# A hybrid SSD and stick-breaking decoder on one core: tiles of 256 tokens behind the attention, 512-column down products, and convolutions that end in their PSUM bank

## The chip, the cores and the metric

The kernel runs on one core of one Trainium2 chip. The metric is the device time of one execution in microseconds (us). It is given as the median of three runs. The profile is of one execution of its own, whose time stands beside the others below.

The engines are named as the profile names them: PE is TensorE (matmuls), PEld its weight loads, DVE is VectorE, ACT is ScalarE, POOL is GpSimd, SP is SyncE (it issues most of the DMAs here).

## The reference

Everything is float32. The stream is 16 learned meta tokens and then 1024 tokens, 1040 in all, of width 1024.

```
h = concat(meta, x)                                        # 1040 x 1024
h = h + ssd_mixer(rmsnorm(h));   h = h + conv_ffn(rmsnorm(h))      # layer 0
k, v = rmsnorm(h) @ w_kv                                   # shared, 16 heads of 64
h = h + stick_breaking_attention(rmsnorm(h) @ w_q, k, v) @ w_o     # layer 1
h = h + conv_ffn(rmsnorm(h))
out = rmsnorm(h)[16:]                                      # the meta tokens are dropped

def conv_ffn(u):                                           # D_FF = 2816
    y = u @ w_up                                           # 2 x 2816 columns
    y = w[0]*y[t-2] + w[1]*y[t-1] + w[2]*y[t] + bias       # causal, 3 taps along the tokens
    g, val = split(y)
    return (silu(g) * val) @ w_down
```

What is returned covers tokens 16 to 1039. The last place where a token mixes with others is the convolution of layer 1's feed-forward part, which looks two tokens back. So behind the attention the result depends on tokens 14 to 1039 alone.

## The kernel before, in words

Tokens lie along the free axis and channels along the 128 partitions, eight channel blocks for the width of 1024. Every float32 product is made of three float32r matmuls (`mm3`, lines 152 to 157): operand and weight are each split into a high and a low part, and high by high, high by low and low by high are added up in one PSUM bank. ACT makes the high parts (a copy with rounding), DVE the operands' low parts and POOL the weights' low parts (both a subtraction with two SBUF inputs).

The stages, in order of time: the mixer of layer 0; `out_proj`, which adds its output to the stream; the feed-forward part of layer 0; the attention; `o_proj`; the feed-forward part of layer 1; the final norm. A feed-forward part has these steps:

- `enter_ffn` (line 726) adds the last part of the projection to the stream in four tiles of `FN` = 260 tokens, squares each row for the norm, and stores the stream in HBM. `forms` (line 804) then makes the normed operands. Both layers work on 1040 tokens. Columns 0 and 1 of each row stand for the two tokens ahead of the first and are zero.
- `up` (line 863) multiplies by a Strassen-like scheme: seven products instead of eight for each of 22 blocks b (a block of gate columns and one of value columns) and each half t of the tokens. Each product is 12 matmuls of 262 columns (a tile and two tokens of halo). The two halves go step by step beside each other. A block holds three PSUM banks, x, y and z. Products 0, 2 and 3 begin them, and DVE adds parts into them in place (line 898). Products 1, 4, 5 and 6 are then accumulated on top. `conv` (line 273) ends each of the four results: ACT multiplies the first tap and adds the bias, and two DVE instructions add the other taps, from the bank into an SBUF tile `c`. For the gate a Silu on ACT follows. `done` (line 889) multiplies gate by value, both in SBUF, on DVE (line 890) and stores the result by DMA. After product 4 the bank y is copied to an SBUF tile by ACT (line 912), and DVE adds two SBUF tiles (line 898) before that result's convolution.
- `down` (line 936) is a Strassen-like scheme as well: two rounds of seven products i, each over two sets of weight rows. For each product `operands` (line 972) makes sums of the stored tiles on DVE and POOL, and splits them (lines 993 to 996). `part` (line 1001) writes eight results, two token tiles t of 260 by four blocks f, into all eight PSUM banks (`kinds`, line 999). The first set starts the eight banks, the second set is accumulated on top, and then `add` (line 1036) takes each bank into an SBUF accumulator, on DVE or, for some first ones, on ACT. Behind the seven products come the last 6 of the 22 weight rows as plain products in four tiles of 260 tokens, and behind each tile `after` is called.
- For layer 1 `after` is `finish` (line 1396): after tiles 1, 2 and 3 it normalises 348, 348 and 344 tokens in chunks of 116 tokens. Each chunk is transposed on PE (eight 128-row blocks, line 1409), scaled on DVE, ACT and POOL, and stored in one DMA whose SBUF side has 116 partitions (112 for the last, 100 for the first) of 4 KB each (line 1448). For the last 344 tokens the sum of squares is taken from the transposed rows (lines 1422 to 1436).

The order of each engine's instructions in these stages is chosen at build time by a scheduler with a model of the times. The attention and the mixer have an order written out by hand. The change touches neither of the two.

Of the kernel before, what the change touches and what calls it, by code (L numbers as in the profile page):

```python
# [13 lines left out]
P = 128  # L14
# [15 lines left out]
FN = 260  # L30
HB = 2
FW = 264

# [35 lines left out]
class Trunk:  # L69
# [99 lines left out]
    def split_half(self, t, s):  # L169

        x = self.Q(s, F32R)
        hi, lo = x[:, : L // 2], x[:, QW // 2 : QW // 2 + L // 2]
# [100 lines left out]
    def conv(self, ps, out, n, taps, halo, wcol, bcol, between=lambda: None):  # L273
# [5 lines left out]
        for i in range(1, taps):  # L279
            nc.vector.scalar_tensor_tensor(out, ps[:, o + i : o + i + n], wcol(i), out, op0=ALU.mult, op1=ALU.add)  # L280
# [94 lines left out]
    def accumulate(self, h, f, s0, n, w, ks, front=0, bank=None, base=0):  # L375

        ps = (bank or (self.ex if f % 3 == 2 else self.mm))("acc")
        c, o = slice(s0 - base, s0 - base + n), slice(front + s0, front + s0 + n)
# [328 lines left out]
    def out_proj(self, hd, ys, yd, pool):  # L707
# [3 lines left out]
        for g in range(3):  # L711
            ops = [self.split(ys[g][q] if yd[g] is None else self.fetch(yd[g][q], "y"), "y") for q in range(4)]
            for f in range(KD):
# [3 lines left out]
                for s0, n in TT:  # L717
                    self.accumulate(h, f, s0, n, lambda i, f: (w[0][:, i * P : i * P + P], w[1][:, i * P : i * P + P]), ops, HB)
        ops = [[self.split_half(ys[3][q][:, L // 2 * x : L // 2 * (x + 1)], "y") for q in range(4)] for x in range(2)]
        ws = [self.load_wd(a["w_out"][12 + i], pool if i < 2 else None) for i in range(4)]  # L720
        return self.enter_ffn(0, h, [(ws, o) for o in ops], pool)
# [4 lines left out]
    def enter_ffn(self, layer, h, last, pool):  # L726


        nc = self.nc
        r = self.rp.tile([P, QW], F32, tag="r", name=self.nm("r"))  # L730
        nc.gpsimd.tensor_copy(r[:, :HB], self.zero[:, :HB])
        d = self.dp.tile([KD, P, L], F32, tag=f"hm{layer}", name=f"hm{layer}")
# [3 lines left out]
        def tile(j, work):  # L736
            ws, ops = last[j // 2]
            ms[j] = self.sm("ms")
            for f in range(KD):
                self.accumulate(h, f, FN * j, FN, lambda i, f: (ws[i][0][:, f * P : f * P + P], ws[i][1][:, f * P : f * P + P]), ops, HB, next(banks), L // 2 * (j // 2))  # L740
                self.square_row(ms[j], h, j, f)
# [3 lines left out]
        def factors(j):  # L745

            c = r[:, HB + FN * j : HB + FN * j + FN]
            b, ps = self.tmp("y")[:, :FN], ms.pop(j)[:, :FN]
# [9 lines left out]
        def rest():  # L758
            forms.append(form_tiles())
            yield from self.forms(h, r, 1, f"ffn_norm{layer}", forms[1][1:], pool)  # L760

        def form_tiles():
# [3 lines left out]
            for x in wide[1]:  # L766
                nc.gpsimd.memset(x.bitcast(F32)[:, HB + 2 * FN : 2 * FW], 0.0)
            own = {i: (self.Q("bh", F32R), self.Q("bl", F32R)) for i in (0, 2, 3, 4, 6)}
            out = {i: [tuple(x[:, k * FW : k * FW + HB + FN] for x in own[i]) for k in range(KD // 2)] for i in own}
            both = [tuple(x[:, k % 2 * 2 * FW : k % 2 * 2 * FW + HB + 2 * FN] for x in wide[k // 2]) for k in range(KD // 2)]  # L770
            out[1] = [tuple(x[:, : HB + FN] for x in hl) for hl in both]
            out[5] = [tuple(x[:, FN :] for x in hl) for hl in both]
            return out, out, both

        def store(x):
            for k in range(KD):
                nc.sync.dma_start(d[k, :, L // 2 * x : L // 2 * (x + 1)], h[k][:, HB + L // 2 * x : HB + L // 2 * (x + 1)])
# [7 lines left out]
        work = self.forms(h, r, 0, f"ffn_norm{layer}", forms[0][1:], pool)  # L785
# [8 lines left out]
    def square_row(self, ms, h, j, f):  # L794

        q = self.tmp("sq")[:, :FN]
        self.nc.scalar.activation(q, h[f][:, HB + FN * j : HB + FN * j + FN], AF.Square)
        self.nc.tensor.matmul(ms[:, :FN], self.ones, q, start=f == 0, stop=f == KD - 1, skip_group_check=True)
# [5 lines left out]
    def forms(self, h, r, t, gain, tiles, pool):  # L804


        nc = self.nc
        N, N2 = HB + FN, HB + 2 * FN
        tt = nc.vector.tensor_tensor
        out, both = tiles  # L810
        s = slice(2 * FN * t, 2 * FN * t + N2)

        new = slice(s.start + HB * t, s.stop)
        for k in range(KD // 2):
# [8 lines left out]
            b11, b12, b21, b22 = b1[:, :N], b1[:, FN:], b2[:, :N], b2[:, FN:]  # L823
# [39 lines left out]
    def up(self, layer, w0, forms, rest, pool):  # L863

        nc = self.nc
        tt = nc.vector.tensor_tensor
        N = HB + FN
# [668 lines left out]
```

## Time and profile before

| | us |
|---|---|
| median of three runs | 3050.51 |
| lowest and highest of them | 3044.32, 3052.45 |
| the profiled execution: its own time | 3047.2 |
| its span, first to last instruction | 3045.5 |

From the trace, the stages run from about 683 to 881 us (`out_proj` with the entry of layer 0's feed-forward part), 912 to 1357 (up, layer 0), 1357 to 1546 (down, layer 0), 1639 to 2176 (the heads of the attention), 2176 to 2312 (`o_proj` and the entry), 2312 to 2756 (up, layer 1), 2756 to 3019 (down, layer 1) and 3019 to 3045.5 (end of the final norm, and the stores).

How to read the views: the page and the groups give busy time of an engine and the mean duration of one instruction. A matmul's duration includes its passage through the array, and matmuls overlap, so what one costs in a row of many is the time of a stretch divided by their number. A table of windows gives the busy time of each engine in chosen stretches, the number of its instructions in brackets, the granted PE clock, and what share of the 16 DMA engines was busy. In a group's last column stands idle time ahead of its instructions and what ended it.

### The profile page before, as it was taken

The page shows a single profiled execution, that of the slowest core. Times are in us where ns is not written, and L with a number is a line of the kernel's source. Part 1 is how long each engine was busy: PE and PEld are TensorE (multiplying, and loading weights), DVE is VectorE, ACT ScalarE, POOL GpSimd, SP SyncE. Part 2 cuts the span into 40 slices and gives each one's busy share as a digit, 9 for nine tenths or more (in the row PEclk, how much of TensorE's full clock was granted, in tenths as well). Part 3 has the DMA queues.
Part 4 walks back from the last instruction along what each step waited for, and adds up shares of the span by engine and source line. Part 5 has one row for each costly group of instructions (what it writes and reads, how often), then busy time and mean ns, then how long its engine had stood idle before and what let it go on. Part 6 is the DMA issues. An engine that isn't in the chain of part 4 may idle for free.

```text
span 3045.5 us, 58682 instructions
## 1 busy us (share of the span) xinstructions
PE 2890.8 (95%) x22535; PEld 2779.1 (91%) x22535; DVE 2336.8 (77%) x4030; ACT 1646.9 (54%) x3403; POOL 1414.2 (46%) x1289
## 2 busy tenths in 40 slices
PE   8999999989989999999999999999998999998996
PEld 5998998889979999999999999999897999998996
DVE  5686868875378888788877888888759877888874
ACT  4555555553246555554335877777645565555332
POOL 1254444532316767657723222222335766666741
PEclk9999999999989999999999999999998999999998
DMA  5243323313212222244132222212431222225231
GB/s 160 74 119 86 110 79 112 111 59 126 80 71 70 79 78 78 83 159 142 50 106 76 63 66 62 57 54 56 150 111 56 74 81 83 77 86 182 71 98 56
DMA packets 125534, 273.42 MB, mean 90 GB/s; under 512 B 15782, under 2 KB 55334, under 8 KB 125254
## 3 DMA queue, kind: packets, MB, share of 16 engines
q1 hardware_dynamic: 119942, 258.74, 27.3%
q10 hardware_dynamic: 4048, 6.36, 0.6%
q0 software_dynamic: 1264, 4.57, 0.4%
q8 instruction: 177, 2.90, 0.4%
q14 instruction: 103, 0.84, 0.1%
HBM read 201.26 MB, written 53.45 MB: 84 GB/s over the span
## 4 chain that ended last, share of the span: by engine, by line
PE 69%; DVE 17%; ACT 5%; issue 5%; POOL 2%; DMA 2%; SPq 0%; POOLq 0%; ACTq 0%; DVEq 0%
PE p L155 9%; PE p L156 9%; PE p L157 9%; PE acc L155 5%; PE pj L155 5%; PE acc L156 5%; PE acc L157 5%; PE pj L156 5%; PE pj L157 5%; DVE gl L996 3%; PE po L1301 2%; PE lg L1259 2%; PE wT L1286 1%; DVE kp L1272 1%; DVE bl L818 1%
## 5 line engine op out<-in xcount | busy, mean ns | idle before, releaser
L155 PE MATMUL pj<-uh,wh 128*128 128x348 f32 (+2 forms) x1536 | 507.5, 331 | 15.9 <-DVE qs L1210 7.1
L156 PE MATMUL pj<-ul,wh 128*128 128x348 f32 (+2 forms) x1536 | 498.9, 325 | 0.0
L157 PE MATMUL pj<-uh,wl 128*128 128x348 f32 (+2 forms) x1536 | 495.6, 323 | 0.0
L156 PE MATMUL p<-bl,fh 128*128 128x262 f32 x1408 | 401.1, 285 | 14.0 <-DVE bl L818 14.0
L155 PE MATMUL p<-bh,fh 128*128 128x262 f32 x1408 | 401.7, 286 | 1.8 <-ACT fh L849 1.4
L157 PE MATMUL p<-bh,fl 128*128 128x262 f32 x1408 | 399.2, 285 | 0.0
L850 POOL TENSOR_TENSOR fl<-x,fh 128x1024 fp32r<-128x1024 f32 x88 | 213.2, 2423 | 352.2 <-ACT fh L849 306.5
L155 PEld LDWEIGHTS pj<-uh,wh 128*128 128x128 f32 x1536 | 291.9, 190 | 23.3 <-DVE qs L1210 9.2
L149 POOL TENSOR_TENSOR wl<-w,wh 128x1024 fp32r<-128x1024 f32 (+2 forms) x80 | 164.1, 2054 | 320.3 <-ACT wh L148 320.1
L156 PE MATMUL p<-bl,wh 128*128 128x262 f32 x1056 | 303.2, 287 | 8.8 <-DVE bl L818 8.8
L155 PE MATMUL p<-bh,wh 128*128 128x262 f32 x1056 | 301.8, 287 | 6.2 <-ACT bh L817 6.2
L157 PE MATMUL p<-bh,wl 128*128 128x262 f32 x1056 | 301.9, 286 | 0.0
L156 PEld LDWEIGHTS pj<-ul,wh 128*128 128x128 f32 x1536 | 292.7, 191 | 1.5 <-issue 0.7
L157 PEld LDWEIGHTS pj<-uh,wl 128*128 128x128 f32 x1536 | 291.9, 190 | 0.2
L280 DVE SCALAR_TENSOR_TENSOR c<-p,params,c 128x260 f32<-128x260 f32 x528 | 251.3, 484 | 48.3 <-ACT c L277 38.5
L156 PEld LDWEIGHTS p<-bl,fh 128*128 128x128 f32 x1408 | 266.9, 190 | 16.0 <-DVE bl L818 15.9
L155 PE MATMUL acc<-gh,wh 128*128 128x260 f32 x896 | 260.5, 291 | 22.1 <-DVE p L1041 10.8
L155 PEld LDWEIGHTS p<-bh,fh 128*128 128x128 f32 x1408 | 267.1, 190 | 4.2 <-ACT fh L849 1.9
L156 PE MATMUL acc<-gl,wh 128*128 128x260 f32 x896 | 259.1, 289 | 11.3 <-DVE gl L996 11.2
L157 PEld LDWEIGHTS p<-bh,fl 128*128 128x128 f32 x1408 | 266.6, 190 | 0.1
L890 DVE TENSOR_TENSOR c<-c,c 128x260 f32<-128x260 f32 x176 | 254.2, 1445 | 6.4 <-ACT c L886 3.4
L157 PE MATMUL acc<-gh,wl 128*128 128x260 f32 x896 | 257.9, 289 | 0.1
(309 smaller groups left out, 8557.4 us busy)
## 6 DMA issues: line engine op xcount, KB each, us to landing
w<-in_w_up SPq DMA_DIRECT2D x88, 512.0 KB
g<-c SPq DMA_DIRECT2D x176, 130.0 KB
w<-in_w_down SPq DMA_DIRECT2D x44, 512.0 KB
w<-in_w_in SPq DMA_DIRECT2D x40, 512.0 KB
b<-g SPq DMA_DIRECT2D x32, 520.0 KB
E<-ea_d SPq DMA_DIRECT2D x32, 464.0 KB
D<-acs_d SPq DMA_DIRECT2D x32, 420.5 KB
h<-h_d SPq DMA_DIRECT2D x16, 520.0 KB
```

The lines of the kernel that those rows point to most:

```text
L149: nc.gpsimd.tensor_tensor(wl[:, :n], w32[:, :n], wh[:, :n].bitcast(F32), op=ALU.subtract)
L155: mm(out, wh, uh, start=first, stop=False, skip_group_check=joins)
L156: mm(out, wh, ul, start=False, stop=False, skip_group_check=joins)
L157: mm(out, wl, uh, start=False, stop=last, skip_group_check=joins)
L280: nc.vector.scalar_tensor_tensor(out, ps[:, o + i : o + i + n], wcol(i), out, op0=ALU.mult, op1=ALU.add)
L818: tt(hl[1], x, hl[0].bitcast(F32), op=ALU.subtract)
L850: tt(lo[:, :n], t, hi[:, :n].bitcast(F32), op=ALU.subtract)
L890: self.last_up = tt(g[:, :FN], g[:, :FN], v[:, :FN], op=ALU.mult)
L996: tt(gl, x, gh.bitcast(F32), op=SUB)
L1259: nc.tensor.matmul(ps[:nt, :m], part[:, c0 : c0 + nt], ks[a][:, s0 : s0 + m], start=x == 0, stop=x == 1)
L1272: nc.vector.tensor_tensor_scan(rev, rev, self.one[:nt].to_broadcast([nt, m + 1]), init, ALU.mult, ALU.mult)
L1301: nc.tensor.matmul(po[64 * a : 64 * a + 64, w], v[: CH[c][1], c, 64 * a : 64 * a + 64], wt[a][: CH[c][1], c, :nt], start=x == 0, stop=x == ...
```

## The change

`FN` becomes `FNS = (260, 256)`, one tile size for each layer's feed-forward part. For layer 0 the tiles stay as they are. For layer 1:

- `o_proj` and everything behind it work on tokens 14 to 1039 (`ORG` = 14). The two columns of halo ahead of the first tile are now tokens 14 and 15 themselves. Tiles are of 256 tokens. In `enter_ffn` the first one has 258. The products of `up` have 258 columns.
- In `down` the two token tiles of 256 become one product of 512 columns (`parts`). Each product i then takes four banks, and `kinds` is cycled, so that consecutive products use different halves of the eight banks.
- `finish` works on 256 tokens, two chunks of 128 tokens, after tile 1 twice, and after tiles 2 and 3. Chunks have 128 partitions. For the last tile all four scalings are on DVE, and each chunk is stored in two DMAs of 512 columns, each behind its own scaling.

For both layers, in `up`: after product 4 DVE adds the bank and the SBUF tile directly, without the copy on ACT. The convolutions of products 5 and 6 end in their own bank (Silu writes it, or the last tap does), and `done` multiplies that bank by an SBUF tile.

```
-FN = 260
+FNS = (260, 256)
+ORG = META - HB
...
-    def conv(self, ps, out, n, taps, halo, wcol, bcol, between=lambda: None):
+    def conv(self, ps, out, n, taps, halo, wcol, bcol, between=lambda: None, last=None):
...
         for i in range(1, taps):
-            nc.vector.scalar_tensor_tensor(out, ps[:, o + i : o + i + n], wcol(i), out, op0=ALU.mult, op1=ALU.add)
+            to = out if last is None or i + 1 < taps else last
+            nc.vector.scalar_tensor_tensor(to, ps[:, o + i : o + i + n], wcol(i), out, op0=ALU.mult, op1=ALU.add)
...
# enter_ffn
-        nc.gpsimd.tensor_copy(r[:, :HB], self.zero[:, :HB])
+        edges = [0] + [HB + F * j for j in range(1, 5)]
+        if layer == 0:
+            edges[0] = HB
+            nc.gpsimd.tensor_copy(r[:, :HB], self.zero[:, :HB])
+        tiles = [(x, y - x) for x, y in zip(edges, edges[1:])]
...
# up
-            def conv(x, i, c):
-                o = self.tmp("c")
-                self.conv(x, o[:, :FN], FN, 3, HB, lambda q: self.par(cw, (KF * i + b) * 3 + q), self.par(cb, KF * i + b))
+            def conv(x, i, back=False):
+
+                o = self.tmp("c")[:, :F]
+                back = x[:, :F] if back else None
+                self.conv(x, o, F, 3, HB, lambda q: self.par(cw, (KF * i + b) * 3 + q), self.par(cb, KF * i + b), last=back if i else None)
                 if i == 0:
-                    nc.scalar.activation(o[:, :FN], o[:, :FN], AF.Silu)
-                return o
-
-            def done(g, v, j):
-                self.last_up = tt(g[:, :FN], g[:, :FN], v[:, :FN], op=ALU.mult)
-                nc.sync.dma_start(d[b, :, FN * j : FN * j + FN], g[:, :FN])
+                    nc.scalar.activation(o if back is None else back, o, AF.Silu)
+                return o if back is None else back
+
+            def done(o, x, y, j):
+                self.last_up = tt(o, x, y, op=ALU.mult)
+                nc.sync.dma_start(d[b, :, F * j : F * j + F], o)
...
-            u3 = copy(product(4, y, False))
-            add(p5, p5, u3)
-            v1 = conv(p5, 1, 1)
+            add(p5, product(4, y, False), p5)
+            v1 = conv(p5, 1)
             yield
-            done(conv(product(5, z, False), 0, 1), v1, 2 * t + 1)
+            done(v1, conv(product(5, z, False), 0, True), v1, 2 * t + 1)
             yield
-            done(g0, conv(product(6, y, False), 1, 0), 2 * t)
+            done(g0, conv(product(6, y, False), 1, True), g0, 2 * t)
...
# down
-        H, S = D // 2, L // 2
+        H, S = D // 2, 2 * F
+        parts = [(0, S)] if S <= 512 else [(0, F), (F, F)]
...
-        kinds = (self.mm, self.sm, self.lg, self.sm, self.mm, self.sm, self.lg, self.ex)
+        kinds = cycle((self.mm, self.sm, self.lg, self.sm, self.mm, self.sm, self.lg, self.ex))
...
-                for n, (t, f) in enumerate((t, f) for t in range(2) for f in range(4)):
+                for t, f in ((t, f) for t in range(len(parts)) for f in range(4)):
                     if x == 0:
-                        ps[t, f] = kinds[n]("acc")
+                        ps[t, f] = next(kinds)("acc")
...
# o_proj
+        spans = (ORG, META + 2 * F), (META + 2 * F, L)
...
-            h[f] = self.fetch(hd[f], "h", front=HB)
+            h[f] = self.Q("h")
+            self.nc.sync.dma_start(h[f][:, : L - ORG], hd[f, :, ORG:])
...
# finish
+        for i in ((0, 1), (2,), (3,))[j]:
+            self.finish_tile(h, i)
...
+        n = FNS[1]
+        s0, last = n * j, j == 3
+        chunks = [(i, s0 + P * i) for i in range(n // P)]
...
-                if b and i < 2:
-                    nc.scalar.activation(y[:m, w], p[:m], AF.Copy, scale=r[:m, i : i + 1])
-                    nc.gpsimd.tensor_tensor(y[:m, w], y[:m, w], self.gfin[:m, w], op=ALU.mult)
+                if b and not last:
+                    nc.scalar.activation(y[:, w], p, AF.Copy, scale=r[:, i : i + 1])
+                    nc.gpsimd.tensor_tensor(y[:, w], y[:, w], self.gfin[:, w], op=ALU.mult)
                 else:
-                    nc.vector.scalar_tensor_tensor(y[:m, w], p[:m], r[:m, i : i + 1], self.gfin[:m, w], op0=ALU.mult, op1=ALU.mult)
-            s = META if t0 == 0 else 0
-            nc.sync.dma_start(out[t0 + s - META : t0 + m - META, :], y[s:m, :])
+                    nc.vector.scalar_tensor_tensor(y[:, w], p, r[:, i : i + 1], self.gfin[:, w], op0=ALU.mult, op1=ALU.mult)
+                if last:
+                    nc.sync.dma_start(out[t0 : t0 + P, w], y[:, w])
+            if not last:
+                nc.sync.dma_start(out[t0 : t0 + P, :], y)
```

More of the change, by code (lines that the diff above doesn't have):

```diff
@@ L759, in rest @@
             forms.append(form_tiles())
-            yield from self.forms(h, r, 1, f"ffn_norm{layer}", forms[1][1:], pool)
+            yield from self.forms(h, r, 1, layer, forms[1][1:], pool)
         def form_tiles():
@@ L784, in enter_ffn @@
         w0 = self.up_weights(layer, 0, pool)
-        work = self.forms(h, r, 0, f"ffn_norm{layer}", forms[0][1:], pool)
+        work = self.forms(h, r, 0, layer, forms[0][1:], pool)
         for j in (2, 3):
@@ L1400, in finish @@
             nc.sync.dma_start(self.gfin, self.a["final_norm"].to_broadcast([P, D]))
[L1401 to L1402 removed]
+        n = FNS[1]
+        s0, last = n * j, j == 3
+        chunks = [(i, s0 + P * i) for i in range(n // P)]
         ss = self.small("fs")
[L1404 to L1406 removed]
+        banks = cycle((self.lg, self.mm) if last else (self.sm,))
@@ L1438, in finish @@
+            nc.vector.tensor_tensor(ss[:, :2], s2[:, 0], s2[:, 1], op=ALU.add)
+            r = self.token_rstd(ss, P, 2)
+        for i, t0 in chunks:
             y = self.Q("y")[:, :D]
```

142 lines of the change are left out of this document (73 added, 69 removed).

## The prediction

> **What bounds the kernel now.** I read the page first, then a table of windows by stage, then the groups with their forms, then single rows.
>
> ```profile
> span 3045.5 us, 58682 instructions
> PE 2890.8 (95%) x22535; PEld 2779.1 (91%) x22535; DVE 2336.8 (77%) x4030; ACT 1646.9 (54%) x3403; POOL 1414.2 (46%) x1289
> PE 69%; DVE 17%; ACT 5%; issue 5%; POOL 2%; DMA 2%; SPq 0%; POOLq 0%; ACTq 0%; DVEq 0%
> ```
> PE is busy nearly all the time and makes up most of the chain; DVE is second. Where each of them binds is seen by stage:
>
> ```profile
> core 0: us, PE busy (x) PEld busy (x) DVE busy (x) ACT busy (x) POOL busy (x), PEclk, DMA share, GB/s
> 690.00:815.00 125.00, 123.37 (x772) 121.52 (x771) 62.75 (x122) 34.82 (x63) 34.69 (x26) 1.00 0.29 100
> 912.00:1355.00 443.00, 442.00 (x3631) 440.57 (x3630) 364.04 (x587) 259.71 (x537) 289.78 (x165) 1.00 0.28 87
> 1357.00:1536.00 179.00, 162.37 (x1284) 159.50 (x1283) 150.13 (x136) 72.78 (x97) 134.75 (x46) 0.96 0.33 106
> 2176.00:2281.00 105.00, 104.82 (x822) 102.34 (x823) 58.11 (x130) 40.91 (x83) 27.32 (x19) 1.00 0.37 129
> 2281.00:2312.00 31.00, 16.75 (x78) 14.24 (x77) 30.86 (x47) 13.85 (x32) 13.90 (x8) 0.67 0.13 43
> 2312.00:2756.00 444.00, 443.16 (x3629) 442.05 (x3628) 362.51 (x587) 260.43 (x534) 290.18 (x165) 1.00 0.27 89
> 2756.00:2936.00 180.00, 163.79 (x1295) 161.12 (x1293) 152.69 (x137) 72.77 (x97) 134.13 (x46) 0.96 0.31 104
> 2936.00:3019.00 83.00, 83.00 (x701) 82.82 (x700) 47.05 (x96) 19.67 (x34) 14.12 (x10) 1.00 0.17 53
> 3019.00:3046.00 27.00, 3.57 (x31) 3.08 (x29) 7.95 (x20) 5.09 (x11) 3.05 (x2) 0.62 0.23 74
> ```
> The stages `out_proj` (first row), `o_proj` (fourth) and both up stages (second and sixth) are full of matmuls: PE busy for 442 of 443 and 443.2 of 444 us. There only fewer PE cycles help, and what DVE or ACT save is worth nothing. The down stages (third and seventh) leave PE idle for 16 to 17 us. Into the norm at 2281 to 2312 DVE leads, and in the last 27 us nothing is busy for long. So the change has to be costed separately in each.
>
> **Narrower tiles, layer 1.** A matmul of 262 columns costs 443.16 / 3629 = 122.1 ns in a row of many (sixth row), one of 348 or 344 columns (346.7 on average) 123.37 / 772 = 159.8 ns (first row). That is 0.445 ns a column. Four columns less save 1.78 ns. The matmuls that it meets, from the code: `o_proj` 480 and its last part in the entry 288, up 22 blocks x 2 halves x 7 products x 12 = 3696, and the six last down rows 576, together 5040, all in stretches that PE fills. 5040 x 1.78 = 9.0 us. The ends are close: 9.4 us if all of the cost goes with the columns, about 7 if the first tile's 258 and waits between products take some back. The DVE-led 31 us shrink with the columns by 4 of 262, 0.5 us.
>
> **Products of 512 columns in layer 1's down stage.** There are 1344 matmuls of 260 columns (2 rounds x 7 x 2 sets x 8 x 6), and there will be 672 of 512. Two of 260 cost 2 x 121.2 = 242.4 ns. By the line through the two rows one of 512 costs 122.1 + 250 x 0.445 = 233.4. The ends are 227.8 (the slope alone, no fixed part) and 238.6 (all in proportion). I take 233.4, as the line holds through 346.7. That is 672 x 9 = 6.0 us of PE time, with ends of 2.6 and 9.8.
>
> The Trainium skill (TensorE: Matmul & The Clock Gate, Back-to-back issue gap) has N / 2.4 + 2.5 ns for a matmul behind another. By it a product of 512 costs 215.8 ns and two of 256 cost 218.3, so joining them would bring next to nothing; the trace disagrees, with 122.1 ns at 262 columns where the rule has 111.7. With 215.8 against the measured pair the sum would have 17.9 us in place of 6.0.
>
> How much of the 6.0 shows depends on what PE waits for in that stage, and on how long DVE takes there:
>
> ```profile
> L155 PE MATMUL acc<-gh,wh 128*128 128x260 f32 x447 | 129.8, 290 | 10.7 <-DVE p L1041 5.4 <-DVE h L1041 3.0 <-DVE c L280 2.2
> L156 PE MATMUL acc<-gl,wh 128*128 128x260 f32 x447 | 128.9, 288 | 5.5 <-DVE gl L996 5.4
> ```
> ```profile
> 2757.00:2805.00 48.00, 40.32 (x303) 39.30 (x302) 46.40 (x19) 23.95 (x41) 43.27 (x14) 0.93 0.29 97
> 2850.00:2897.00 47.00, 41.63 (x339) 40.80 (x338) 45.79 (x46) 17.14 (x17) 41.49 (x13) 0.98 0.04 12
> ```
> PE waits 16 us in all: 8.4 for a bank that DVE has not yet added up (L1041), 2.2 for one that a last convolution still reads (L280), 5.4 for a low part (L996). In the first half of each round (95 us) DVE is busy for 46.4 of 48 and 45.8 of 47 us and leads; in the rest PE does. In the PE-led 84 us the wider products bring 6.0 x 84 / 179 = 2.8 us, and the four free banks end the 3.0 us of waits for `h`. In the DVE-led part only DVE's savings count. They come from here:
>
> ```profile
> L890 DVE TENSOR_TENSOR c<-c,c 128x260 f32<-128x260 f32 x176 | 254.2, 1445 | 6.4 <-ACT c L886 3.4
> L898 DVE TENSOR_TENSOR ft<-ft,ft 128x262 f32<-128x262 f32 x88 | 86.0, 977 | 0.1
> L898 DVE TENSOR_TENSOR p<-p,ft 128x262 f32<-128x262 f32 x176 | 72.9, 434 | 61.2 <-ACT ft L895 60.4 <-PE p L157 0.7
> L1041 DVE TENSOR_TENSOR h<-h,acc 128x260 f32<-128x260 f32 x112 | 42.8, 416 | 11.2 <-PE acc L157 11.2
> L630 DVE TENSOR_TENSOR state<-state,S 128x512 f32<-128x512 f32 x28 | 19.0, 679 | 3.7 <-POOL state L629 3.7
> ```
> The same amount of work takes 1445 or 977 ns with both inputs in SBUF and 434 or 416 with one in PSUM. What stretches it is seen at the turn from up to down, first DVE, then POOL:
>
> ```profile
> 2758.43 4.95 DVE L890 TENSOR_TENSOR c<-c,c 128x260 f32<-128x260 f32 x2 [1.68 <-ACT c L886]
> 2763.30 1.00 DVE L280 SCALAR_TENSOR_TENSOR c<-p,params,c 128x260 f32<-128x260 f32 x2
> 2764.33 1.56 DVE L890 TENSOR_TENSOR c<-c,c 128x260 f32<-128x260 f32 x1
> 2765.81 2.38 DVE L979 TENSOR_TENSOR b<-b,b 128x1040 f32<-128x1040 f32 x2
> ```
> ```profile
> 2758.16 2.40 POOL L994 TENSOR_TENSOR wl<-w,wh 128x1024 fp32r<-128x1024 f32 x1 [18.40 <-ACT wh L993]
> 2760.53 2.55 POOL L978 TENSOR_TENSOR w<-w,w 128x1024 f32<-128x1024 f32 x1
> 2763.05 2.56 POOL L994 TENSOR_TENSOR wl<-w,wh 128x1024 fp32r<-128x1024 f32 x1
> ```
> Each multiply ends where a POOL subtraction ends (2760.5, 2763.1, 2765.6). With an input in PSUM they don't wait for POOL.
>
> **The turn from up to down.** The three last multiplies take 6.5 us and would take 3 x 0.42, so DVE comes to its first sum (L979) up to 5.2 us earlier, in both layers. In layer 0 that is all that is gained. PE cannot use all of it, since POOL's three subtractions end at 2765.6 as before: I take 4 us, between 0 and 5.2. In layer 1 the DVE-led part gets the 5.2, and from the second round's four products in it 4 x (8 x 0.416 - 4 x 0.679) = 2.5 us, and 0.5 from 1024 columns in place of 1040. Sum for layer 1's down stage: 2.8 + 3.0 + 5.2 + 2.5 + 0.5 = 14. Waits that end for one reason come back in part as waits for the low parts, so I take 12, between 4 and 17.
>
> **The up stages themselves.** Of a layer's 88 multiplies each sheds 1.0 us of DVE, of its 44 additions each 0.55, and 44 copies leave ACT. All of it lies beside PE, which has no idle time to give: 0. What could cost something is that banks y and z are now held until the multiply. `s` and `t` go in turns, 14 products of 12 x 0.122 = 1.46 us for a pair. Bank y of `s` is released behind its product 6 (13th place) and is taken again, with three buffers, 15 products after its product 2 (18th place): four products, 5.9 us, lie between. The chain in it is ACT 0.57, two taps of 0.48 and a multiply of 0.42, some 2 us. z has more room. So 0; below is the price if the cover is gone. Nothing is queued behind these waits on PE but the next product 2.
>
> **The end.** Only the last tile's norm and stores lie behind the last matmul:
>
> ```profile
> 3019.78 0.43 DVE L382 TENSOR_TENSOR h<-h,acc 128x260 f32<-128x260 f32 x1 [1.73 <-PE acc L157]
> 3021.48 1.29 DVE L1430 COPY copy<-fin 116x512 f32<-116x512 f32 x2 [1.28 <-PE fin L1409]
> 3025.43 0.16 DVE L1435 TENSOR_TENSOR fs<-fs 128x3 f32<-128x3 f32 x1
> 3027.10 2.07 DVE L1446 SCALAR_TENSOR_TENSOR y<-fin,ty,gfin 116x512 f32<-116x512 f32 x3
> ```
> ```profile
> 3029.20 3.54 SPq L1448 DMA_DIRECT2D out<-y  x3
> ```
> ```profile
> 2273.00:2275.00 2.00, 2.00 (x17) 1.94 (x17) 2.00 (x7) 0.72 (x3) 0.00 (x0) 1.00 0.77 294
> 3030.00:3044.00 14.00, 0.00 (x0) 0.00 (x0) 0.00 (x0) 0.00 (x0) 0.95 (x1) 0.50 0.34 100
> ```
> ```profile
> 2922.26 3.72 DMA g<-g
> ```
> Two chunks in place of three take a copy and a square from DVE (0.65 each): L1435 comes at 3024.1 instead of 3025.4. The small chain to the first scaling takes 1.7 as before: 3025.8. Four scalings of 0.69 end at 3028.6. Stores of 116 and 112 partitions run at 100 GB/s in the last 14 us with 0.34 of the DMA engines; the stream's stores of 128 partitions (2273 to 2275) run at 294 GB/s with 0.77. So the last 256 KB, issued at 3028.9, take about what a read of 260 KB over 128 partitions takes, 3.7 us: 3032.6. With 1 us for the close (an estimate: 14 us at 100 GB/s are the 1.4 MB stored and end at about 3044, the span at 3045.5) it is 3033.5 instead of 3045.5: 12 us less. SP's ten stores instead of nine cost nothing, as its first six are issued beside matmuls. Eight transposes less save 0.9 us of PE (0.11 each).
>
> **Sum.** 9.0 + 0.5 + 12 + 4 + 12 + 0.9 = 38 us. The span goes from 3045.5 to 3007, the profiled execution from 3047.2 to 3009. The median is 3.3 above that execution: 3050.5 - 38 = 3012.5.
>
> **Rivals.**
> - Slower: the banks of the up stages. If the multiply into y ends later than the 5.9 us after product 6, PE waits once for each of 42 blocks and layer. From 0.45 us of lateness on (84 x 0.45 = 38) all is given back; 1 us gives 3012.5 + 84 = 3096. Against it: the chain of 2 us, and a DVE that gets freer. 5%.
> - The down stage stays with DVE and POOL: their subtractions go on in turns, PE's 16 us of waits only change place, and layer 0 gains nothing. Then 16 of the 38 shrink to 3: 3025. For it: POOL's 43.3 of 48 us. 20%.
> - The end: 100 GB/s belongs to the output tensor, not to 116 partitions. Then 1 MB takes 10.5 us from 3027 on and the end saves 7 instead of 12: 3017. 10%. The Trainium skill (DMA: Bandwidth & Descriptors, Why a DMA increments its semaphore by 16 and not by 1) says that a DMA uses the largest number of engines up to 16 that divides its outer dimension. By it 116 partitions use 4, and 128 use 16; no run here has yet shown it for this output.
> - A product of 512 columns costs 216 ns, with a fixed part that vanishes: 672 x 17.4 more PE time goes, half of it in the PE-led part: 3007. 5%.
>
> **How the numbers follow.** My forecast has 60%: 3012, with its own range of 3004 to 3020 from the ends of the terms. With the rivals the range is 2998 to 3032: the lower end takes the upper ends of all the terms and the cheap product, the upper end the second and third rival together. What a measurement can tell from no change is 0.3%, 9 us. All but the first rival lie under 3041: faster 0.93, the same 0.03, slower 0.04.
>
> **What would show it.** In the changed profile: up of layer 1 shorter by 6.6 us and that of layer 0 by none, PE still full in both; L890 near 420 ns; about 672 products of 512 columns, at about 233 ns in a full stretch; waits for L1041 nearly gone; behind the last product 14 us instead of 26, with stores that use most DMA engines. I would be wrong if PE waited for DVE inside the up stages, or if the down stage kept its 180 us.

## The result, and the profile after

The changed kernel takes 3025.11 us (median of four runs, 3024.58 to 3029.16) against 3050.51: a ratio of 0.9924, with an interval of 0.9909 to 0.994. (The 3050.51 is a median of four runs as well, and not of three.) It is 25 us faster, where 38 were predicted.

The page of the kernel after, in the lines that answer to those of before:

```profile
span 3023.1 us, 57199 instructions
PE 2875.1 (95%) x21855; PEld 2733.1 (90%) x21855; DVE 2158.8 (71%) x3994; ACT 1621.9 (54%) x3308; POOL 1403.3 (46%) x1282
PE 52%; DVE 13%; ACT 4%; issue 3%; DMA 2%; POOL 0%; SPq 0%; DVEq 0%; ACTq 0%; POOLq 0%
```
DVE lost 178 us of work, POOL 11, PE 16. Only 22.4 us of span went between the two profiled executions (3 us less than between the medians, so 3 of the 25 us stand in no row below), and most of DVE's saving lay beside PE. Where the span went is seen by stage. The table of windows after, cut at the first and last matmul of each stage (busy us of each engine, instructions in brackets, then granted clock, DMA share, GB/s); in order: layer 0's seven products; its last six weight rows with the way to the attention's heads; `o_proj`; the entry; up; layer 1's seven products; its last six rows; the end.

```profile
1356.70:1544.00 187.30, 168.84 (x1347) 166.36 (x1346) 155.74 (x148) 74.50 (x100) 139.37 (x48) 0.96 0.32 107
1544.00:1641.30 97.30, 92.12 (x696) 89.75 (x695) 62.99 (x108) 34.50 (x69) 24.82 (x19) 0.96 0.26 86
2178.00:2281.60 103.60, 103.44 (x819) 101.13 (x819) 56.68 (x128) 40.19 (x83) 26.63 (x19) 1.00 0.37 128
2281.60:2312.00 30.40, 16.11 (x80) 13.46 (x78) 30.26 (x45) 13.22 (x28) 14.31 (x8) 0.66 0.15 49
2312.00:2752.90 440.90, 438.95 (x3634) 438.02 (x3635) 271.22 (x592) 248.74 (x494) 283.83 (x165) 1.00 0.27 90
2752.90:2925.90 173.00, 160.65 (x674) 127.02 (x673) 157.29 (x99) 70.05 (x82) 136.72 (x46) 0.98 0.31 103
2925.90:3011.50 85.60, 80.19 (x652) 79.57 (x651) 52.91 (x102) 22.64 (x46) 18.64 (x15) 0.96 0.17 67
3011.50:3023.10 11.60, 1.64 (x16) 1.40 (x13) 6.58 (x17) 3.07 (x7) 0.00 (x0) 0.74 0.24 90
```
The same stages before, cut in the same way:

```profile
1356.10:1544.70 188.60, 171.34 (x1346) 168.47 (x1345) 157.03 (x150) 75.49 (x101) 138.34 (x48) 0.95 0.34 110
1544.70:1639.10 94.40, 91.02 (x694) 88.92 (x693) 63.50 (x108) 34.31 (x69) 24.41 (x19) 0.98 0.27 88
2175.80:2280.40 104.60, 104.42 (x822) 101.84 (x819) 57.71 (x130) 40.30 (x83) 26.72 (x19) 1.00 0.37 127
2280.40:2312.00 31.60, 17.35 (x82) 14.84 (x81) 31.46 (x49) 14.45 (x32) 14.50 (x8) 0.68 0.14 49
2312.00:2756.30 444.30, 443.46 (x3632) 442.35 (x3631) 362.77 (x588) 260.43 (x534) 290.18 (x165) 1.00 0.27 89
2756.30:2942.70 186.40, 170.19 (x1347) 167.34 (x1346) 157.14 (x146) 75.11 (x100) 136.53 (x47) 0.96 0.32 106
2942.70:3019.60 76.90, 76.90 (x652) 76.90 (x651) 42.34 (x87) 17.33 (x31) 11.72 (x9) 1.00 0.14 45
3019.60:3045.50 25.90, 2.97 (x26) 2.48 (x24) 7.95 (x20) 5.09 (x11) 3.05 (x2) 0.61 0.24 75
```
Row by row, before less after: +1.3 and -2.9 in layer 0's down stage, +1.0 `o_proj`, +1.2 the entry, +3.4 up of layer 1, +13.4 its seven products, **-8.7 its last six rows**, +14.3 the end. That is 23.0; the stages not shown give -0.6. (Of the -2.9 about half or less repeats: `e3_two_of_256` and `e10_last_product_256` below, with the same layer 0, take 95.9 and 95.5 us there.) The row to explain is the seventh: 652 matmuls that PE did without a gap before now take 8.7 us longer. PE's waits there, by line and releaser (us in all, times, longest), after:

```profile
PE acc L156 <- DVE h L1054: 3.4, 2, 2.0
PE acc L158 <- POOL wl L1063: 2.0, 1, 2.0
```
Before, the same view is empty. The waits bring 5.4 us; the rest goes with the clock, 0.96 in that row against 1.00 (last section).

### The profile page after: what moved, and what is told of

It reads as the page before. It is cut to its first block, busy times and chain, and to the rows that moved or that the text cites. A ratio compares the mean times of both kernels' runs of the same rounds, so it can differ in the third digit from the quotient of the medians.

```text
span 3023.1 us, 57199 instructions
## 1 busy us (share of the span) xinstructions
PE 2875.1 (95%) x21855; PEld 2733.1 (90%) x21855; DVE 2158.8 (71%) x3994; ACT 1621.9 (54%) x3308; POOL 1403.3 (46%) x1282
## 4 chain that ended last, share of the span: by engine, by line
PE 52%; DVE 13%; ACT 4%; issue 3%; DMA 2%; POOL 0%; SPq 0%; DVEq 0%; ACTq 0%; POOLq 0%
PE p L156 9%; PE p L157 9%; PE p L158 9%; PE acc L157 4%; PE acc L156 4%; PE acc L158 4%; DVE gl L1007 3%; PE po L1314 2%; PE pj L156 2%; PE pj L158 2%; PE pj L157 2%; PE lg L1272 1%; DVE kp L1285 1%; PE wT L1299 1%; ACT kp L1275 1%
## 5 line engine op out<-in xcount | busy, mean ns | idle before, releaser
L157 PE MATMUL p<-bl,fh 128*128 128x262 f32 (+1 forms) x1408 | 401.0, 285 | 14.0 <-DVE bl L827 14.0
L156 PE MATMUL p<-bh,fh 128*128 128x262 f32 (+1 forms) x1408 | 401.3, 286 | 4.2 <-ACT fh L858 3.5
L158 PE MATMUL p<-bh,fl 128*128 128x262 f32 (+1 forms) x1408 | 399.3, 284 | 0.0
L157 PE MATMUL p<-bl,wh 128*128 128x262 f32 (+1 forms) x1056 | 301.8, 286 | 8.5 <-DVE bl L827 8.5
L156 PE MATMUL p<-bh,wh 128*128 128x262 f32 (+1 forms) x1056 | 301.9, 286 | 6.3 <-ACT bh L826 6.3
L158 PE MATMUL p<-bh,wl 128*128 128x262 f32 (+1 forms) x1056 | 301.2, 285 | 0.0
L282 DVE SCALAR_TENSOR_TENSOR c<-p,params,c 128x260 f32<-128x260 f32 (+1 forms) x440 | 207.9, 481 | 94.4 <-ACT c L278 92.6
L157 PE MATMUL acc<-gl,wh 128*128 128x260 f32 (+1 forms) x672 | 217.9, 326 | 19.8 <-DVE gl L1007 19.8
L384 DVE TENSOR_TENSOR h<-h,acc 128x256 f32<-128x256 f32 (+4 forms) x232 | 102.6, 450 | 175.1 <-PE acc L158 172.5
L156 PE MATMUL acc<-gh,wh 128*128 128x260 f32 (+1 forms) x672 | 215.0, 325 | 8.7 <-DVE p L1054 5.4
```

The lines of the kernel that those rows point to most:

```text
L156: mm(out, wh, uh, start=first, stop=False, skip_group_check=joins)
L157: mm(out, wh, ul, start=False, stop=False, skip_group_check=joins)
L158: mm(out, wl, uh, start=False, stop=last, skip_group_check=joins)
L282: nc.vector.scalar_tensor_tensor(to, ps[:, o + i : o + i + n], wcol(i), out, op0=ALU.mult, op1=ALU.add)
L384: self.nc.vector.tensor_tensor(h[f][:, o], h[f][:, o], ps[:, :n], op=ALU.add)
```

## The experiments

**Which half of the change acts.** Two kernels take it apart. `e1_convs_only` is the kernel before with the new `up` alone (`conv` with `last`, no copy, `done` with a bank); `e2_tiles_only` is the kernel after with the old `up` and its copy.

> The kernel before with the PSUM convolutions alone, in both layers, tiles as before. Theory (DVE reaches its first sum of the down stage 5 us earlier, but then takes turns with POOL and the low parts come no earlier): 3049 to 3051 of 3050.5, no change; L890's successor near 430 ns, L979's successor 5 us earlier in both layers, PE's waits in the two down stages still 15 to 17 us each. Rival (what the prediction had: the head start reaches PE): 4 to 5 us less in each layer, 3041.

> The changed kernel with the convolutions as before (copies, multiplies in SBUF), tiles of 256, 512-column products and the new end kept. Theory: 3024 to 3028, the same as the changed kernel within 3 us, since the up stages are full of matmuls and the turn gives nothing. Rival (the convolutions carry part of the gain): 3033 or more.

Measured: `e1_convs_only` 3048.63 us, ratio 1.0002 (0.9993 to 1.0012); `e2_tiles_only` 3025.29, ratio 0.9927 (0.9913 to 0.9942). Neither theory is contradicted: the gain comes from the tiles, the products and the end. The convolutions that end in PSUM take nearly all of the 92 us that DVE lost in layer 1's up stage (362.8 to 271.2 in the rows above), and nothing that shows from the kernel.

**The wide products alone.** The kernel after, with products of two times 256 columns again:

```
-        parts = [(0, S)] if S <= 512 else [(0, F), (F, F)]
+        parts = [(0, F), (F, F)]
```


> The changed kernel with two products of 256 columns in place of one of 512 in layer 1's down stage, all eight banks for each product. Theory: the seven-product part gets 5 to 8 us longer (672 x 9 ns, and waits for banks), and 3 to 5 us of the waits in the last six rows go, as PE comes there later: 3027 to 3029. Rival (the wide products cause the waits, with adds of 0.68 us): the last six rows lose all 8.7 us that they had gained, and the kernel comes to 3020 or less.

Measured: 3025.51 us, ratio 0.9921 (0.9905 to 0.9938): no difference to after. The seven products of `e3_two_of_256` and its last rows:

```profile
2751.20:2935.90 184.70, 165.53 (x1346) 163.05 (x1346) 152.95 (x145) 74.27 (x100) 139.62 (x47) 0.97 0.32 104
2935.90:3012.80 76.90, 76.49 (x652) 76.28 (x651) 45.89 (x95) 21.49 (x44) 14.94 (x13) 1.00 0.14 56
```
The products of 512 columns do save 11.7 us in the first row (184.7 to 173.0), and lose 8.7 in the second (76.9 to 85.6). The gain is real, and most of it is given back at once. Theory and rival each had one half: the rows get all of their 8.7 us back, as the rival said, but the products lose more than the 5 to 8 us of the theory, so the kernel stays above the rival's 3020.

**The end.** The kernel before, with only its stores cut so that most of each has 112 partitions (seven times sixteen), and the other 4 follow:

```
-            nc.sync.dma_start(out[t0 + s - META : t0 + m - META, :], y[s:m, :])
+            for a, b in ((s, 112), (112, m)) if m > 112 else ((s, m),):
+                nc.sync.dma_start(out[t0 + a - META : t0 + b - META, :], y[a:b, :])
```


> The kernel before with each store of 116 partitions cut into one of 112 and one of 4. Theory (the number of partitions sets how many DMA engines work): the last stores use most engines, about 300 GB/s instead of 100, and the time behind the last matmul falls from 26 to 17 or 18 us: 3042. Rival (100 GB/s belongs to the output): 3050 or a little more.

Measured: 3035.97 us, ratio 0.996 (0.9946 to 0.9975), and 17.2 us behind the last matmul instead of 25.9. The trace puts 8.7 us of the gain there, as the theory had it; the 2.4 us of span besides lie in stages that the edit leaves alone. The DMA view of the last microseconds, 40 slices each: first the kernel before (slices of 0.44 us), then `e4_store_112` (0.36), then after (0.35):

```profile
DMA  0000135799733343222313222232222211010000
GB/s 0 0 0 0 66 84 159 178 243 215 131 94 75 103 122 94 84 84 94 56 66 94 94 94 94 103 112 94 84 103 103 84 66 56 37 47 9 0 0 0
```
```profile
DMA  0000000000000000000009997999999976200000
GB/s 0 0 0 0 0 0 0 0 0 0 0 0 0 0 0 0 0 0 0 0 0 319 307 273 262 296 307 307 273 273 296 353 307 239 80 23 0 0 0 0
```
```profile
DMA  0000000000000000000000000002999999960000
GB/s 0 0 0 0 0 0 0 0 0 0 0 0 0 0 0 0 0 0 0 0 0 0 0 0 0 0 0 105 392 375 380 375 375 381 386 228 0 0 0 0
```
The first digit row sits at 2 to 3 tenths of the 16 engines for most of the way, the other two at 9. (Its hump of up to 243 GB/s was not taken apart; the last of its three stores has 112 partitions.) Before and in `e4_store_112` it is the same tensor in the same rows of 4 KB, and only the cut by partitions differs: some 95 GB/s with 116, some 300 with 112. After, with 128 and rows of 2 KB, it is 380. The rival, that the slow rate belongs to the output, falls. The Trainium skill (DMA: Bandwidth & Descriptors, Why a DMA increments its semaphore by 16 and not by 1) gives the largest divisor up to 16: 4 engines for 116, 16 for 112 and 128; the trace agrees, with 2 to 3 tenths of the engines busy in the one case and 9 in the others.

**Why the last six rows lose 8.7 us: first tries.** I took POOL's late low parts and DVE's sums at that place for the cause, each curable by itself: `e5a_stage_only` gives every second of the six weight rows a staging buffer of its own, `e5b_sums_later` has the program write the sums (L1024) one for each row product in the first tile, and two in the second; `e5_stage_and_sums` does both.

```
+            if b % 2:
+                w32 = pool.tile([P, QW], F32, tag="x32", name=self.nm("x32"), bufs=2)[:, :D]
...
-                for _ in range(2 if j == 0 else 1):
+                for _ in range(2 if j == 1 else 1):
```


> The changed kernel, and in both layers' down stages every second of the last six weight rows is staged in the other tile kind (x32) instead of all in the three of w32, and the second share of the sums of accumulators is taken one tile later. Theory (the last six rows wait for their weights' low parts, which queue for staging tiles and take turns with DVE, and for adds that queue behind the sums): layer 1's last six rows fall from 85.6 to 77 to 80 us, the kernel to 3016 to 3020. Rival (the loss there has another cause, the halved clock at any short wait, or the width of the adds alone): 3024 or more.

> The changed kernel with the second kind of staging tile alone. Theory: PE's wait of 2.0 us for a weight's low part at the head of the last six rows goes, with one interval of half clock: 3 to 4 us of the 8.7, kernel about 3021. Rival (POOL's pace, not the staging, sets it): 3024 to 3026, the wait as before.

> The changed kernel with the later sums alone. Theory: the waits for banks that DVE has not added up (1.4 and 2.0 us, with an interval of half clock) go: 3 to 5 us, kernel about 3021. Rival (the adds are late because of the low parts ahead of them, not the sums): 3024 to 3026.

Measured: 3027.16, 3026.3 and 3025.48 us, ratios 0.9933 (0.9916 to 0.9949), 0.9929 (0.9914 to 0.9944) and 0.9928 (0.9913 to 0.9944). None differs from after: all three theories missed, and the times are about those of their rivals. In `e5a_stage_only` PE's waits stayed (3.5 us for `h`, 2.1 for POOL's low part), so a staging buffer of its own is no cure. In `e5b_sums_later` the scheduler put the sums where they had been, so it tested nothing, and `e5_stage_and_sums` only the staging: here, writing the sums later in the program did not move them.

**Whether DVE and POOL bind the seven products.** The kernel after without POOL's sums of weight tiles in `operands`; it leaves these four sums out of each set, in both layers:

```
-                    pt(a21, a11, a21, op=SUB)
-                    pt(a21, a22, a21, op=SUB)
-                    pt(a11, a11, a21, op=ADD)
-                elif i == 3:
-                    pt(a21, a12, a21, op=SUB)
```


> The changed kernel without POOL's sums of weights in both down stages (left out: the four sums of weight tiles in operands, for each set; the products then work on unsummed weights). Theory (DVE and POOL take turns on operations with SBUF inputs, so each POOL operation of 2.4 us delays DVE's low parts): DVE's low parts fall from 2.4 us towards 1.2, PE's waits in the first half of each round go, the seven-product part of layer 0 falls from 187 to about 175 and that of layer 1 from 173 to about 160: kernel 2997 to 3005. Rival (DVE's own number of operations is the bound): under 5 us in each layer, 3016 or more.

Measured: 2984.21 us, ratio 0.9794 (0.9779 to 0.9808), more than expected. Its seven products of layer 1:

```profile
2730.50:2887.40 156.90, 156.26 (x674) 126.11 (x674) 131.63 (x101) 71.12 (x83) 82.00 (x32) 1.00 0.35 121
```
PE is now full (156.26 of 156.9 us), and DVE, whose own instructions were not touched, is busy for 131.6 us instead of 157.3. 55 us of POOL's time gone shorten DVE's by 26: POOL's operations had stretched DVE's. PE's waits in these products, after:

```profile
PE acc L157 <- DVE gl L1007: 9.8, 4, 4.9
PE acc L158 <- POOL wl L1005: 2.4, 2, 1.9
```
They are for low parts, most of them DVE's (L1007), and in `e6_no_pool_sums` 0.6 us of them is left. The run lightens POOL's own load and DVE's stretching at once and doesn't tell the two apart. Its last six rows still take 83.4 us, with 4.3 us of waits for `h`: POOL's low parts at that place were left in. The row above also prices a product of 512 columns: 156.26 / 674 = 231.8 ns.

**The last rows again: sums, low parts, or grain.** Three more kernels, all from the one after. `e7_rows_no_low` leaves out the low parts of the last six weight rows, `e8_sums_behind` moves the sums in the scheduler's order and not in the text, `e10_last_product_256` gives the last product alone the finer grain:

```
# e7_rows_no_low
-            pt(lo, w32, hi.bitcast(F32), op=SUB)
-            ws.append((hi, lo))
+            ws.append((hi, hi))
# e8_sums_behind
-                tt(x, x, ps[:, :n], op=ADD)
+                self.last_add = tt(x, x, ps[:, :n], op=ADD)
...
-                        tt(acc[x, f], acc[x, f], acc[y, f], op=ADD)
+                        behind(tt(acc[x, f], acc[x, f], acc[y, f], op=ADD), self.last_add, "behind the adds")
# e10_last_product_256
+            if last and i == 2:
+                parts[:] = [(0, F), (F, F)]
```


> The kernel after, in which the last six weight rows of the down stage have no low part (GpSimd's subtraction L1063 is left out in both layers and the high part stands in its place; the output is therefore without these low parts). Theory: the last six rows of layer 1 take 85.6 us instead of 76.9 because GpSimd's low parts L1063 (2.4 to 2.9 us each) and VectorE's operations at that place slow each other, and the adds of the last product come up to 11 us late. Without L1063 the rows take 76 to 79 us and the kernel 3014 to 3019. Rival: the loss is VectorE's own load (adds, sums and roundings of the token tiles), or the clock that falls to one half by its own; then the rows stay at 83 us or more and the kernel at 3022 or more.

> The kernel after, in which VectorE's 28 sums L1024 of both layers may only start behind the last add L1054 of product 2; in the kernel after 12 of them stand ahead of it. Theory: TensorE's waits for h (1.4 and 2.0 us at the start of the last six rows) come from adds that queue behind these sums, and each brings an interval of half clock with it; with the sums behind the adds the waits go, the rows of layer 1 take 79 to 82 us and the kernel 3018 to 3022. The wait of 2.0 us for GpSimd's low part stays. Rival: the adds are late for the operations that GpSimd slows and not for the sums, or the sums then delay the row's own adds; the rows stay at 84 to 88 us and the kernel at 3024 to 3028.

> The kernel after, in which the last product (product 2 of the last round, both sets) of layer 1 goes in two parts of 256 columns again, all other products in one of 512. Theory (VectorE's load decides, not the grain of the work): the adds are 8 times two of 0.41 us instead of 8 of 0.67 us, so VectorE has 1 us more to do and the rows stay at 84 to 88 us; the kernel takes 3024 to 3028. Rival: the grain decides, since an add of 512 columns frees its bank and its h only when all of the product is done; then the rows take 78 to 81 us and the kernel 3017 to 3021.

Measured: 3009.11 (ratio 0.9866, 0.9851 to 0.9881), 3015.1 (0.9886, 0.9871 to 0.9901) and 3025.09 us (0.992, 0.9904 to 0.9937). In the first two the last rows take 78.1 and 80.1 us, as the theory had it, and the kernel is 5 and 3 us below its range; layer 0's seven products gain as well (182.2 and 182.9 us instead of 187.3). The third is at the expected time, but by another way: its rows take 76.4 us, its seven products 182.7, with PE's waits now inside the product:

```profile
PE acc L156 <- DVE h L1054: 5.8, 4, 2.4
```
The grain only chooses where PE meets the wait. What DVE is busy with decides. The groups of the sixteen sums into `h` (busy us, mean ns of one) over layer 1's down stage, before, and after:

```profile
L1012 DVE TENSOR_TENSOR h<-h,p 128x520 f32<-128x520 f32 x16 | 14.4, 923 | 0.0
```
```profile
L1024 DVE TENSOR_TENSOR h<-h,p 128x512 f32<-128x512 f32 x16 | 17.4, 1105 | 0.1
```
The same sums on fewer columns take 3.0 us more. That alone is not the 8.7 that the rows lost: it matters which operations are stretched and what stands behind them. DVE and POOL at that place, after, tell it (start, duration, in us; of DVE's lines five are left out, between 2933.7 and 2936.2):

```profile
2925.09 2.29 DVE L1024 TENSOR_TENSOR h<-h,p 128x512 f32<-128x512 f32 x1
2927.30 0.67 DVE L1054 TENSOR_TENSOR h<-h,acc 128x512 f32<-128x512 f32 x1
2927.90 2.84 DVE L1024 TENSOR_TENSOR h<-h,p 128x512 f32<-128x512 f32 x2
2930.67 0.67 DVE L1054 TENSOR_TENSOR h<-h,acc 128x512 f32<-128x512 f32 x1
2931.38 2.43 DVE L1024 TENSOR_TENSOR h<-h,p 128x512 f32<-128x512 f32 x1
2936.73 0.67 DVE L1054 TENSOR_TENSOR h<-h,acc 128x512 f32<-128x512 f32 x1
2937.32 0.68 DVE L1024 TENSOR_TENSOR h<-h,p 128x512 f32<-128x512 f32 x1
```
```profile
2921.61 7.98 POOL L1063 TENSOR_TENSOR wl<-w,wh 128x1024 fp32r<-128x1024 f32 x3 [1.06 <-ACT wh L1062]
2930.88 2.37 POOL L1063 TENSOR_TENSOR wl<-w,wh 128x1024 fp32r<-128x1024 f32 x1 [1.29 <-ACT wh L1062]
```
A sum with two SBUF inputs takes 0.68 us once POOL is done (2937.3), and 2.3 to 2.4 while POOL subtracts; the add from PSUM between them takes 0.67 either way. The token tiles' low parts on DVE are stretched in the same way (two of them take 5.30 us from 2913.0 on, beside POOL, and 0.68 each from 2933.7 on). The last adds, which PE waits for, stand in DVE's queue behind such operations, and the last one ends at 2937.4; PE had issued its last product at 2925.6. Taking POOL's work away (`e7_rows_no_low`) or the sums out of its time (`e8_sums_behind`) brings back 7.5 and 5.5 of the 8.7 us.

**The version that beats both.** In `e8_sums_behind` nine sums stood ahead of the first row add, and PE waited 2.7 us there. One more assignment keeps the program's order, one row add, then two sums:

```
# accumulate, on top of e8_sums_behind
-        self.nc.vector.tensor_tensor(h[f][:, o], h[f][:, o], ps[:, :n], op=ALU.add)
+        self.last_add = self.nc.vector.tensor_tensor(h[f][:, o], h[f][:, o], ps[:, :n], op=ALU.add)
```


> The kernel of the run in which VectorE's 28 sums L1024 stand behind the last add of product 2, and each of them now also behind the last add L384 of the row products that the program wrote ahead of it, so that VectorE's order is one row add, two sums, one row add, as the program has it. In the run before, nine sums stood ahead of the first row add, and TensorE waited 2.7 us for the bank that this add frees, with 3.4 us of full-speed records in a row behind it. Theory: the wait is that order alone; it goes, the rows of layer 1 take 76 to 78 us instead of 80.1, and the kernel is 1 to 4 us under the run before: 3010 to 3015. Rival: VectorE's load decides (rounding of the token tiles, sums and adds fill its time to the heads of the output), so the wait comes back later in the rows; the kernel takes 3015 to 3018.

Measured: 3005.85 us (3004.53 to 3007.73), ratio 0.9858 (0.9841 to 0.9874): the wait is gone, and 9 us with it, more than the 1 to 4 expected. (That expectation's clause on full speed only says that no half clock followed the wait.) Its last six rows, and its sixteen sums into `h` over layer 1's down stage:

```profile
2915.20:2991.70 76.50, 76.50 (x651) 76.50 (x650) 52.43 (x109) 21.87 (x45) 15.92 (x14) 1.00 0.16 60
```
```profile
L1027 DVE TENSOR_TENSOR h<-h,p 128x512 f32<-128x512 f32 x16 | 12.2, 763 | 0.0
```
A sum takes 763 ns on average instead of 1105, PE has no gap in 76.5 us, and the clock stays at 1.00. The order holds for layer 0 as well, and the surplus lies there: of the 10.8 us of span between this kernel and `e8_sums_behind`, 9.3 are in layer 0's down stage and the way to the heads (272.8 instead of 282.1). PE's waits there fall by 7.4 us, from 22.5 to 15.1: 2.1 for a row add (L384), 2.0 for `h` and 2.0 for DVE's low parts are the largest that go. Why the waits for low parts shrink was not taken apart. Nor was this order tried on the kernel before.

## Why the prediction was right and wrong

3025.1 lies in the range, but the likeliest case, 3012 with its own 3004 to 3020, did not come. The rival "the down stage stays with DVE and POOL" gave 3025, with 3 us left of the 16 for the two down stages; measured are 6.0, or 3.1 with the -2.9 of layer 0's last rows. Its reason, that DVE and POOL go on in turns, is what the runs show: PE's idle time in layer 1's down stage goes from 16.2 to 12.4 us in the seven products and from 0 to 5.4 in the rows behind them. That its number is met so well is in part luck: the narrower tiles gave 4 us less than said, the end gave more, and 3 us of the 25 are the distance of the profiled executions from their medians.

- **Narrower tiles: 8.5 said, 5.6 measured** in `o_proj`, entry and up. (For the last rows another 1.0 was said; `e11_sums_spread`, where PE has no gap there, takes 76.5 us against 76.9 before.) The slope was too steep. In a full stretch of layer 1's up stage, before and then after:

```profile
2400.00:2700.00 300.00, 300.00 (x2467) 300.00 (x2466) 242.44 (x383) 174.69 (x354) 205.73 (x120) 1.00 0.24 79
```
```profile
2400.00:2700.00 300.00, 300.00 (x2494) 300.00 (x2494) 179.09 (x389) 165.83 (x327) 202.95 (x120) 1.00 0.24 79
```
 300 / 2467 = 121.6 ns and 300 / 2494 = 120.3: four columns are worth 1.3 ns and not 1.78, so 3696 matmuls give 4.8 us and not 6.6. PE's idle time in the stage also rose from 0.8 to 2.0 us. A slope from 262 to 347 columns didn't carry down to 258.
- **A product of 512 columns: right.** 231.8 ns in `e6_no_pool_sums`, between the ends and close to the 233.4 that was taken. What it brought was undersized: the terms that hang on it (2.8 for PE's time, 3.0 for the banks, 2.5 for the adds) make 8.3 us, and taking the wide products back costs the seven products 11.7 (`e3_two_of_256`). The isolated-matmul rule of the Trainium skill (TensorE: Matmul & The Clock Gate, Back-to-back issue gap) gives 215.8 and is not met here.
- **Layer 1's down stage: 12 said, 4.7 measured** (263.3 to 258.6 us for the two rows together). The step that failed is that nothing behind the seven products would be late: the prediction let waits come back only inside them. PE came to the last rows 13.4 us earlier in the stage, DVE's last adds then stood behind operations that POOL's low parts stretched, and 8.7 us went there. That the seven products alone gave 13.4, close to what was said, is luck: the 5.2 us of the turn did not come (next point), and the wide products gave more than their share.
- **The turn: 4 said in layer 0, 1.3 measured; 5.2 said in layer 1, next to none.** This is the other step that failed. The multiplies did get cheap, as the group after shows, and the first sum began 5.6 us earlier (L990 at 1361.2, L979 at 1366.8 before). DVE and then POOL after it, after:

```profile
L901 DVE TENSOR_TENSOR c<-p,c 128x260 f32<-128x260 f32 x88 | 37.3, 424 | 2.3 <-ACT p L897 0.6
```
```profile
1361.20 6.16 DVE L990 TENSOR_TENSOR b<-b,b 128x1040 f32<-128x1040 f32 x2
1370.61 3.39 DVE L1007 TENSOR_TENSOR gl<-b,gh 128x1040 fp32r<-128x1040 f32 x1
```
```profile
1362.85 3.41 POOL L1005 TENSOR_TENSOR wl<-w,wh 128x1024 fp32r<-128x1024 f32 x1
1366.34 3.25 POOL L992 TENSOR_TENSOR w<-w,w 128x1024 f32<-128x1024 f32 x1
```
 The two sums that took 2.38 us before now take 6.16, because they run beside POOL, and from then on both engines go in pairs of 3.3 to 3.4 us (alone, an operation of DVE takes 1.2 and one of POOL 2.4). The first low part ends at 1374.0, 17.3 us into the stage, against 17.6 before. DVE's head start was spent on waiting for POOL. Layer 1 does the same. Its first low part ends at 2772.7 before, 16.4 us into the stage, and at 2769.9 after, 17.0 us into it; the lines, before and then after:

```profile
2769.27 3.43 DVE L996 TENSOR_TENSOR gl<-b,gh 128x1040 fp32r<-128x1040 f32 x1
```
```profile
2766.56 3.37 DVE L1007 TENSOR_TENSOR gl<-b,gh 128x1024 fp32r<-128x1024 f32 x1
```
 With the convolutions alone (`e1_convs_only`) layer 1's seven products take 185.9 us against 186.4:

```profile
2755.40:2941.30 185.90, 168.88 (x1347) 166.61 (x1346) 152.44 (x148) 74.09 (x100) 140.12 (x47) 0.96 0.32 104
```
 The prediction saw that a multiply with two SBUF inputs ends with POOL's subtraction, but let the sums behind it, which have two SBUF inputs as well, keep the 1.2 us each that they took before. They took it because POOL then stood idle for 3.57 us, as POOL's line before shows:

```profile
2769.18 2.43 POOL L994 TENSOR_TENSOR wl<-w,wh 128x1024 fp32r<-128x1024 f32 x1 [3.57 <-ACT wh L993]
```
 Moved ahead, they run beside POOL. (With the wide products in place the convolutions do shorten the seven products, from 175.6 in `e2_tiles_only` to 173.0 us, but not the kernel.)
- **The end: 12.9 said with the transposes, 14.3 measured.** Mechanism right, the stores faster than said: 380 GB/s, so the last data are out some 2 us behind the last scaling, and not 3.7 and the close.
- **The up stages: right.** `e1_convs_only` gave 1.0002; the rival with the banks did not come.

## What to carry to other kernels

When an engine gets faster, look at what its saved time is filled with: an instruction that moves forward may land beside another engine that stretches it. Place work with two SBUF inputs on VectorE where GpSimd is idle, by an order that the scheduler must keep, and not by the text. And cut stores so that their partition count is a multiple of sixteen before changing anything else: here two lines took 8.7 of the 14.3 us from the end.

## What the runs showed of the hardware

That DVE and POOL share time was known from the profile before; the price was not. An operation of 0.68 us costs DVE 2.2 to 2.4 us while POOL subtracts, one of 1.2 costs 3.4, and the add with one PSUM input keeps its 0.67. The Trainium skill (SBUF — State Buffer, Who interferes with whom) has it as a lock held for a whole instruction, by whichever engine starts first: the trace agrees as to the whole instruction, as operations of 1.2 and 2.4 us start every 3.3 to 3.4 us in turn, so that hardly anything of them overlaps. Short waits of PE can cost more than themselves: in the last six rows after, its waits of 1.4 and 2.0 us are followed by 3.7 and 3.4 us with a granted clock of 0.54 and 0.50 (the 1.4 comes 0.4 us behind the wait of 2.0 for POOL's low part), as the windows show:

```profile
2931.40:2935.10 3.70, 3.70 (x18) 3.70 (x19) 3.70 (x4) 1.26 (x2) 1.85 (x1) 0.54 0.11 43
2938.50:2941.90 3.40, 3.40 (x18) 3.40 (x17) 1.91 (x6) 0.00 (x0) 0.00 (x0) 0.50 0.00 0
```
At half clock that is another 1.7 us each: 5.4 us of waits and 3.4 of clock make up the 8.7. Not every wait brings such a stretch: `e8_sums_behind` waited 2.7 us once in its last six rows, and their granted clock reads 1.00.
